# Mixed block pair with routed experts, 256 tokens: the first gather of the experts' stage spread over the first group's products, filler products during the routing, row splits on VectorE, one more weight tile

## The chip, the cores and the metric

The program runs on one core of a Trainium2 chip. TensorE (PE) multiplies, with its weight loads listed apart as PEld; VectorE (DVE), ScalarE (ACT) and GpSimd (POOL) do elementwise work; SyncE's queue (SP) issues the DMAs. The metric is the device time of one execution in microseconds (us), and the median of the runs counts. A profile is one further execution, recorded instruction by instruction.

## The reference

Two transformer blocks on 256 tokens of width 2048, all in float32. The first has two recurrent mixers, cross-attention and an MLP; the second has a gated mixer and, at the end, routed experts. Only the end matters for this change:

```python
x = x + gate1 * (y @ w_out[l])                       # end of the second mixer
h = rms_norm(x, norm2_g[l]) * (1.0 + scale2) + shift2
m = hierarchical_moe(h, ...)                         # 256 rows
x = x + gate2 * m

def hierarchical_moe(h, ...):                        # cut
    g_logits = hf @ w_group + b_group                # 4 groups, top 1
    e_logits = hf @ w_route + b_route                # 8 experts of that group, top 2
    weights = softmax(top_val) * p_group
    # rows sorted by expert; for each expert e and its rows xb:
    act = silu(xb @ w_gate[e]) * (xb @ w_up[e])      # 2048 -> 256
    ys = act @ w_down[e]                             # 256 -> 2048
    # out[n] = sum over its 2 experts of weights * ys
```

There are 32 experts with 2048x512 gate and up weights and 256x2048 down weights each. That is 6 MB an expert, so 192 tiles of 1 MB (128x2048 float32) are read.

## The kernel before

The stages run one after another: mixers, output product, cross-attention, MLP, the second block's mixer (`block2`), and the experts (`moe`). This text is about the seam between the last two and about `moe`.

**Routing and rows.** `route_piece` turns the rows of `h` into logits while `block2`'s last product ends. `moe` starts with `row_bcast` (32 small products that spread `gate2` over the partitions) and `route`, a long chain of short VectorE instructions: maxima, one-hots, counts by a few products of ones, ranks `rm`, weights `W`. `onehot` (L1639) makes from `rm` a matrix `oh` that picks the rows of a group of experts. `rows_hilo` normalizes the rows and splits them into `xh` (rounded, on ScalarE, L1656) and the remainder `xl`. For the first 128 tokens the remainder is made on GpSimd (L1661 and L1662), for the second 128 on VectorE (L1658). It does this for four column quarters q, so there are 8 `xh` and 8 `xl` instructions in all.

**Gather.** `gather` returns 8 pieces. Piece j makes two of the 16 column chunks of the gathered, transposed rows `xs`: eight products with `xh` and `xl` into one PSUM tile `mx` (two buffers), one drain on ScalarE (L1513) and one on VectorE (L1511). 

**Groups.** The 32 experts are in 9 groups, in most of which four experts have 32 rows each; such a group's four products sit side by side in TensorE's columns. `experts_in` makes gate and up of a group in four steps kg, one weight tile an expert in each. `experts_mid` applies the nonlinearity (L1579 to L1586) and `experts_out` makes the down products (tiles in two halves), scales them (L1610), splits them, and adds them to `h` (L1620). A float32 product appears in the trace as several instructions; a step kg of a four-expert group as 32, four at a time.

**Which expert is where.** The first group holds experts 0 to 3, whatever the routing. From the second group on, the experts stand in the order of their row counts, which `order` works out: some 16 VectorE instructions over 128x1024 elements (L1439 to L1446). It needs two work tiles `at` and `pr` of the tag `wh`, which has three buffers; its result `ids` (L1451) is read by SP's queue for the addresses of all loads from tile number 24 on.

**Weight tiles.** `load_ahead` issues the 192 loads in the order of their use, from SP's queue (L1714, L1721). Tiles 5, 6 and 7 go once into spare memory (an `xs` buffer and `wh`, `wl` buffers); the other tiles go round a ring of 9 slots: two in `b`, three `raw`, four `mw`. A load waits until the products on its slot's previous tile are done, and `take`, called before each kg and each half of the down products, issues what has become free by then. So 12 tiles are loaded ahead of the first group: its steps kg 0 to 2.

**Order of instructions.** The source is a sequence, and a scheduler decides at build time in which order each engine gets its instructions: the earlier in the source the higher the priority, but an instruction that the scheduler takes to be ready goes ahead of one that it takes to be waiting. On the chip each queue then runs in that fixed order. `keep_in_program_order` pins an instruction behind the one traced last on its engine.

Of the kernel before, what the change touches and what calls it, by code (L numbers as in the profile page):

```python
# [11 lines left out]
F32 = mybir.dt.float32  # L12
# [4 lines left out]
ALU = mybir.AluOpType  # L17
# [165 lines left out]
class Prog:  # L183
# [1463 lines left out]
    def rows_hilo(self, P):  # L1647
        nc = self.nc
        self.xh, self.xl = self.b16(F32R), self.b16(F32R)

        rs2 = self.smp.tile([128, 2], F32, tag="rs2", name="rs2", bufs=1)
        self.tc.keep_in_program_order(nc.vector.tensor_copy(rs2, self.rs))
        for q in range(4):
            for tb in range(2):
                c = self.cols(q)
                nc.scalar.activation(self.xh[:, tb, c], self.h[:, tb, c], AF.Copy, scale=self.rs[:, tb:tb + 1])  # L1656
                if tb:
                    nc.vector.scalar_tensor_tensor(self.xl[:, tb, c], self.h[:, tb, c], rs2[:, tb:tb + 1], self.xh[:, tb, c], ALU.mult, ALU.subtract)  # L1658
                else:
                    v = P.tile([128, 512], F32, tag="ey", name="xn", bufs=2)  # L1660
                    nc.gpsimd.tensor_scalar(v, self.h[:, tb, c], self.rs[:, tb:tb + 1], None, ALU.mult)  # L1661
                    nc.gpsimd.tensor_tensor(self.xl[:, tb, c], v, self.xh[:, tb, c], ALU.subtract)  # L1662


    def weights_init(self):
# [20 lines left out]


    def slot_tile(self, P, i):
        k = i % 9
        if k < 2:  # L1690
            if i == 0:
                self.pair = self.b16()
            w = self.pair[:, k]
        elif k < 5:
            w = self.rawp.tile([128, 2048], F32, tag="raw", name="raw")
        else:
            w = P.tile([128, 2048], F32, tag="mw", name="mw", bufs=4)
        return w

    def spare_tile(self, P, k):  # L1700
# [7 lines left out]
    def load_ahead(self, n, P=None):  # L1708
        while len(self.issued) < min(n, len(self.loads)):
            j = len(self.issued)  # L1710
            if 5 <= j < 8:
                w = self.spare_tile(P, j - 5)
                for x in range(2):
                    self.nc.sync.dma_start(w[x], self.loads[j]()[:, x * 1024:x * 1024 + 1024])  # L1714
            else:
                i = j if j < 5 else j - 3
                if (j - 12 if j < 17 else j - 9) >= self.used:
                    break
                w = self.slot_tile(P, i)
                if j < len(self.loads) - 4:  # L1720
                    self.nc.sync.dma_start(w, self.loads[j]())  # L1721
                w = self.halves(w)
            self.issued.append(w)

            if j == len(self.loads) - 1:
                for x in range(2):
                    for y in range(j - 3, j + 1):
                        self.nc.sync.dma_start(self.issued[y][x], self.loads[y]()[:, x * 1024:x * 1024 + 1024])
# [16 lines left out]
    def moe(self):  # L1745
        nc = self.nc
        with ExitStack() as ctx:
# [2 lines left out]
            self.row_bcast(self.modc[:, 5], self.g2row)  # L1750
            K = ctx.enter_context(self.tc.tile_pool(name="kept", bufs=1))
            P = ctx.enter_context(self.tc.tile_pool(name="moe", bufs=1))
            self.load_ahead(12, P)
            self.route(K)

            oh = self.onehot(P, [0], self.rm)
            self.rows_hilo(P)
            xs, work = self.gather(P, oh, 128)
            for w in work:
                w()  # L1760
            self.order(K)
            last = len(GROUPS) - 1
            st = self.group_in(P, 0, xs, oh, self.W, [[]] * 4)
            self.group_out(P, 0, st)
            oh = self.onehot(P, [1, 2], self.rmo)
            xs, work = self.gather(P, oh, 256)
# [3 lines left out]
            for g in range(1, last + 1):  # L1770
                i = (g - 1) % 2
                work = [[], [], [], []]
# [6 lines left out]
                c = slice(i * 128, i * 128 + 128)  # L1779
                st = self.group_in(P, g, [x[:, c] for x in xs], oh[:, :, c], self.Wo, work)  # L1780
# [5 lines left out]
                if i:  # L1786
                    oh, xs = oh2, xs2
            self.group_out(P, last, prev, last=True)
            n = nc.values_load(self.nov[0:1, 0:1], min_val=0, max_val=15)
            with self.tc.For_i(0, n, 1):  # L1790
                x = self.extra(P)
                xo, work = self.gather(P, x[0], 64)
                for w in work:
                    w()

                def load(src):
                    w = P.tile([128, 2048], F32, tag="mw", name="mw", bufs=4)
                    nc.sync.dma_start(w, src)
                    return self.halves(w)

                gu = lambda kg: [load(self.ins["wgu"][bass.ds(self.xe, 1), kg].rearrange("o p a c -> (o p) (a c)"))]
                halves = iter(range(2))
                dn = lambda: [load(self.ins["wd"][bass.ds(self.xe, 1), next(halves)].rearrange("o p c -> (o p) c"))]
                self.experts_out(P, self.block_in(P, gu, xo, *x), dn, last=True)
# [55 lines left out]
```

## Time and profile before

| | us |
|---|---|
| median of 3 runs | 2320.45 |
| lowest, highest | 2318.12, 2325.05 |
| the profiled execution | 2339.39 |
| its span | 2337.3 |

The profiled execution took 18.9 us more than the median; its span leaves out 2.1 us around the recorded work. Times inside the profile are counted from the span's start. An engine's busy time says little by itself; what matters is which wait ends last at each point.

### The profile page before, as it was taken

What the parts mean: (1) busy time and instruction counts of PE and PEld (TensorE: products, weight loads), DVE (VectorE), ACT (ScalarE), POOL (GpSimd) and SP (SyncE); (2) the same over time, 40 slices, a digit from 0 to 9 for tenths busy, and PEclk for the clock granted to TensorE, in tenths of its full rate; (3) what the DMA queues carried; (4) which work ended last, traced back from release to release, by engine and by line L of the source; (5) the groups of instructions that cost most, each with busy time, mean ns of one, the idle gap of its engine ahead of it and who ended that gap; (6) DMA issues with size and microseconds to landing.
All of it is one profiled execution on the core that took longest, in us unless ns stands there. A gap on an engine that the chain in (4) does not pass through costs nothing.

```text
span 2337.3 us, 40924 instructions
## 1 busy us (share of the span) xinstructions
PE 2198.2 (94%) x16672; PEld 1705.7 (73%) x16672; DVE 1507.6 (65%) x2557; ACT 893.2 (38%) x1445; POOL 70.6 (3%) x174
## 2 busy tenths in 40 slices
PE   6999999999999989999999999999999789888877
PEld 6988888888887779998998988987987432233222
DVE  5778887757678788777787787767657622222223
ACT  5444443444544445444444434445555210011000
POOL 1000000010000000000000000000000100000000
PEclk9999999999899999999999999999999799999999
DMA  7425443233268777887786787754445698999998
GB/s 244 150 94 179 157 164 130 82 105 110 73 234 303 284 274 258 278 306 267 264 315 248 261 318 258 260 186 153 166 161 196 250 386 336 405 388 420 420 421 336
DMA packets 101622, 575.18 MB, mean 246 GB/s; under 512 B 11548, under 2 KB 12700, under 8 KB 45880
## 3 DMA queue, kind: packets, MB, share of 16 engines
q1 hardware_dynamic: 101432, 572.55, 65.4%
q8 instruction: 132, 2.16, 0.4%
q14 instruction: 58, 0.48, 0.1%
HBM read 570.40 MB, written 2.10 MB: 245 GB/s over the span
## 4 chain that ended last, share of the span: by engine, by line
PE 78%; DMA 10%; DVE 8%; ACT 2%; issue 2%; SPq 0%; DVEq 0%; ACTq 0%
PE acc L250 44%; PE mx L250 32%; DMA mw<-wgu 3%; PE mx L254 2%; DMA raw<-wgu 2%; DMA raw<-wd 1%; DVE wl L290 1%; DMA mw<-wd 1%; DVE macc L830 1%; DMA mraw<-wmod 1%; DMA row<-wmod 1%; DMA b<-wgu 0%; DMA raw<-wout 0%; ACT wh L289 0%; DVE pr L1445 0%
## 5 line engine op out<-in xcount | busy, mean ns | idle before, releaser
L289 ACT CAST wh<-raw 128x1024 fp32r<-128x1024 f32 (+1 forms) x496 | 516.7, 1044 | 722.1 <-PE acc L250 517.4
L290 DVE TENSOR_TENSOR wl<-raw,wh 128x1024 fp32r<-128x1024 f32 (+1 forms) x496 | 599.9, 1214 | 202.3 <-ACT wh L289 199.9
L250 PE MATMUL acc<-b,wh 128*128 128x256 f32 x2560 | 467.5, 284 | 1.0 <-ACT b L367 1.0
L250 PE MATMUL mx<-b,wh 128*128 128x256 f32 (+1 forms) x2016 | 419.4, 298 | 0.7 <-ACT wh L289 0.7
L250 PEld LDWEIGHTS acc<-b,wh 128*128 128x128 f32 x2560 | 396.5, 189 | 3.2 <-ACT b L367 1.7
L250 PE MATMUL acc<-b,wl 128*128 128x256 f32 x1280 | 362.0, 283 | 0.0
L250 PEld LDWEIGHTS mx<-b,wh 128*128 128x128 f32 (+1 forms) x2016 | 324.4, 193 | 11.9 <-issue 3.3
L250 PE MATMUL mx<-b,wl 128*128 128x256 f32 (+1 forms) x1008 | 300.0, 298 | 0.3 <-DVE wl L290 0.3
L250 PEld LDWEIGHTS acc<-b,wl 128*128 128x128 f32 x1280 | 243.2, 190 | 0.7 <-DVE wl L290 0.4
L830 DVE SCALAR_TENSOR_TENSOR macc<-mraw,silc,macc 128x1024 f32<-128x1024 f32 x160 | 205.0, 1282 | 58.0 <-DMA mraw<-wmod 57.5
L250 PE MATMUL acc<-wh,fh 128*128 128x512 f32 x512 | 199.8, 390 | 0.0
L250 PE MATMUL acc<-wl,fh 128*128 128x512 f32 x512 | 199.6, 390 | 0.0
L250 PE MATMUL acc<-wh,fl 128*128 128x512 f32 x512 | 199.2, 389 | 0.0
L250 PEld LDWEIGHTS mx<-b,wl 128*128 128x128 f32 (+1 forms) x1008 | 193.5, 192 | 4.8 <-DVE wl L290 0.8
L250 PE MATMUL mx<-mw,xs 128*32 128x512 f32 (+1 forms) x448 | 127.5, 649 | 15.3 <-DMA mw<-wgu 15.3
L250 PE MATMUL acc<-wh,b 128*128 128x512 f32 x384 | 124.8, 403 | 1.0 <-ACT row L971 1.0
L250 PE MATMUL mx<-raw,xs 128*32 128x512 f32 (+1 forms) x344 | 105.7, 646 | 12.4 <-DMA raw<-wgu 12.4
L250 PEld LDWEIGHTS acc<-wl,fh 128*128 128x128 f32 x512 | 96.1, 188 | 20.8 <-DVE wl L290 1.0
L250 PEld LDWEIGHTS acc<-wh,fl 128*128 128x128 f32 x512 | 96.1, 188 | 19.8
L250 PEld LDWEIGHTS acc<-wh,fh 128*128 128x128 f32 x512 | 96.1, 188 | 19.8
L250 PE MATMUL mx<-b,xs 128*32 128x512 f32 (+1 forms) x240 | 92.1, 722 | 12.5 <-DMA b<-wgu 12.5
L1580 DVE SCALAR_TENSOR_TENSOR eth<-eth,mx 128x256 f32<-128x256 f32 x9 | 3.8, 421 | 150.5 <-ACT eth L1579 150.5
(481 smaller groups left out, 2802.0 us busy)
## 6 DMA issues: line engine op xcount, KB each, us to landing
raw<-w SPq DMA_DIRECT2D x128, 1024.0 KB, 5.7
mraw<-wmod SPq DMA_DIRECT2D x160, 512.0 KB, 5.0
raw<-win SPq DMA_DIRECT2D x76, 1024.0 KB, 4.8
mw<-wgu SPq DMA_DIRECT2D x54, 1024.0 KB, 11.0
raw<-wgu SPq DMA_DIRECT2D x42, 1024.0 KB, 12.3
b<-wgu SPq DMA_DIRECT2D x29, 1024.0 KB, 12.6
mw<-wd SPq DMA_DIRECT2D x26, 1024.0 KB, 12.3
raw<-wout SPq DMA_DIRECT2D x24, 1024.0 KB, 5.3
```

The costliest lines, as they stand in the source:

```text
L250: return self.nc.tensor.matmul(out, lhsT=lhsT, rhs=rhs, start=start, stop=stop, skip_group_check=True)
L254: return self.nc.tensor.transpose(out, in_, self.ident[:k, :k])
L289: nc.scalar.copy(h[:, :n], rs)
L290: nc.vector.tensor_tensor(l[:, :n], rs, h[:, :n], ALU.subtract)
L830: nc.vector.scalar_tensor_tensor(a, b, self.silc[:, k:k + 1], a, ALU.mult, ALU.add)
L1580: nc.vector.scalar_tensor_tensor(th[:n], th[:n], 1.0, ps[:n, 0:256], ALU.add, ALU.mult)
```

## The change

In `rows_hilo` all 8 remainders are made on VectorE; the 8 GpSimd instructions go. Ahead of them 8 products of ones with a constant (128x128 by 128x256, result unused) are put into TensorE's queue behind the routing's products. The ring gets a tenth slot, a fifth `mw` tile, and 13 tiles are loaded ahead, so the first tile of the first group's kg 3 is among them. The first gather's pieces no longer all stand ahead of the first group: pieces 0 and 1 stand ahead of kg 0, 2 and 3 ahead of kg 1, 4 and 5 ahead of kg 2, 6 and 7 and then `order` ahead of kg 3.

```diff
         self.tc.keep_in_program_order(nc.vector.tensor_copy(rs2, self.rs))
+        self.busy(8)
         for q in range(4):
             for tb in range(2):
                 c = self.cols(q)
                 nc.scalar.activation(self.xh[:, tb, c], self.h[:, tb, c], AF.Copy, scale=self.rs[:, tb:tb + 1])
-                if tb:
-                    nc.vector.scalar_tensor_tensor(self.xl[:, tb, c], ...)
-                else:
-                    v = P.tile([128, 512], F32, tag="ey", name="xn", bufs=2)
-                    nc.gpsimd.tensor_scalar(v, self.h[:, tb, c], self.rs[:, tb:tb + 1], None, ALU.mult)
-                    nc.gpsimd.tensor_tensor(self.xl[:, tb, c], v, self.xh[:, tb, c], ALU.subtract)
+                nc.vector.scalar_tensor_tensor(self.xl[:, tb, c], self.h[:, tb, c], rs2[:, tb:tb + 1], self.xh[:, tb, c], ALU.mult, ALU.subtract)
+    def busy(self, n):
+        ps = self.acc()
+        for _ in range(n):
+            self.tc.keep_in_program_order(self.mm(ps[:, 0:256], self.ones, self.c("run")))
...
-        k = i % 9
+        k = i % 10
...
-            w = P.tile([128, 2048], F32, tag="mw", name="mw", bufs=4)
+            w = P.tile([128, 2048], F32, tag="mw", name="mw", bufs=5)
...
-                if (j - 12 if j < 17 else j - 9) >= self.used:
+                if (j - 13 if j < 18 else j - 10) >= self.used:
...
-            self.load_ahead(12, P)
+            self.load_ahead(13, P)
...
             xs, work = self.gather(P, oh, 128)
-            for w in work:
-                w()
-            self.order(K)
             last = len(GROUPS) - 1
-            st = self.group_in(P, 0, xs, oh, self.W, [[]] * 4)
+            work.append(lambda: self.order(K))
+            st = self.group_in(P, 0, xs, oh, self.W, [work[0:2], work[2:4], work[4:6], work[6:9]])
```

## Rows read from the trace of the kernel before

**Rows 1.** The page: mean busy tenths of the DMA engines over 40 slices of the span.
```profile
DMA  7425443233268777887786787754445698999998
```

**Rows 2.** Busy time by stretch; the last three columns: TensorE's clock, DMA share, GB/s.
```profile
1826.00:1846.00 20.00, 19.64 (x88) 14.02 (x92) 5.57 (x12) 3.66 (x8) 0.00 (x0) 0.51 0.13 55
1900.00:1904.40 4.40, 4.40 (x37) 2.23 (x37) 0.55 (x1) 0.57 (x1) 0.00 (x0) 1.00 0.25 54
1949.00:1972.50 23.50, 22.46 (x90) 6.32 (x92) 5.11 (x16) 2.91 (x6) 0.00 (x0) 1.00 0.58 221
1996.00:2000.00 4.00, 4.00 (x44) 1.21 (x39) 0.00 (x0) 0.00 (x0) 0.00 (x0) 1.00 0.52 180
2048.00:2054.60 6.60, 6.60 (x62) 2.47 (x64) 0.00 (x0) 0.00 (x0) 0.00 (x0) 1.00 0.39 117
2054.60:2313.00 258.40, 216.31 (x1020) 67.55 (x1013) 67.25 (x119) 22.72 (x42) 0.00 (x0) 0.96 1.01 421
```

**Rows 3.** SP's queue in order of time: start, us, the loads issued.
```profile
1815.01 2.10 SPq L1721 DMA_DIRECT2D mw<-wgu  x4
1846.11 1.14 SPq L1721 DMA_DIRECT2D b<-wgu  x2
...
1863.70 11.75 SPq L1721 DMA_DIRECT2D raw<-wgu  x2
```

**Rows 4.** TensorE in order of time at the first group: start, us, count, idle before.
```profile
1813.95 3.92 PE L250 MATMUL mx<-cst,modc 128*128 128x128 f32 x32
1820.15 1.05 PE L250 MATMUL mx<-route,cst 128*128 128x64 f32 x8 [2.28 <-DVE route L1392]
...
1826.36 2.40 PE L250 MATMUL mx<-oh,b 128*128 128x128 f32 x10 [1.84 <-DVE b L1658]
...
1830.53 10.50 PE L250 MATMUL mx<-oh,b 128*128 128x128 f32 x48
...
1849.74 3.59 PE L250 MATMUL mx<-mw,xs 128*32 128x512 f32 x28
...
1858.37 0.62 PE L250 MATMUL mx<-raw,xs 128*32 128x512 f32 x1 [1.46 <-DMA raw<-wgu]
...
1868.80 0.69 PE L254 MATMUL mx<-cst,ea 128*128 128x128 f32 x2 [6.81 <-DVE ea L1582]
1870.00 1.06 PE L250 MATMUL acc<-raw,eat 128*32 128x512 f32 x1 [0.52 <-DVE eat L1586]
```

**Rows 5.** TensorE's clock as it fell: length, PE, PEld, DVE, ACT, POOL, clock, DMA.
```profile
1818.00:1822.00 4.00, 1.05 (x8) 0.97 (x8) 3.79 (x12) 3.32 (x7) 3.80 (x4) 0.97 1.02 414
1822.00:1826.00 4.00, 1.51 (x6) 1.35 (x6) 4.00 (x11) 0.43 (x1) 3.75 (x3) 0.50 1.01 426
```

**Rows 6.** VectorE in order of time: routing, `rs2`, then `order`.
```profile
1817.36 1.29 DVE L1412 TENSOR_TENSOR route<-route 128x8 f32<-128x8 f32 x1
...
1820.59 0.97 DVE L1417 TENSOR_TENSOR route<-route 128x8 f32<-128x8 f32 x1
...
1822.28 0.16 DVE L1418 TENSOR_TENSOR route<-route 128x8 f32<-128x8 f32 x1
...
1823.30 1.24 DVE L1652 COPY rs<-rs_y 128x2 f32<-128x2 f32 x1
...
1848.66 1.23 DVE L1439 TENSOR_TENSOR pr<-order 128x1024 f32<-128x1024 f32 x1 [6.69 <-PE mx L250]
...
1855.01 0.18 DVE L1451 CAST ids<-idf 128x32 int32<-128x32 f32 x1
...
1867.14 1.21 DVE L1446 TENSOR_REDUCE order<-pr 128x32 f32<-128x1024 f32 x1
```

**Rows 7.** By source line: a VectorE instruction like a remainder's, min/median/max in ns.
```profile
L1202 DVE SCALAR_TENSOR_TENSOR h<-h,rfr,xg x8: 741/745/747, 1761.3 to 1778.7; 128x512 f32<-128x512 f32 x8
```

**Rows 8.** TensorE's waits for weight tiles after the pauses of the stream.
```profile
1921.47 1.92 PE L250 MATMUL mx<-mw,xs 128*32 128x512 f32 x2 [1.44 <-DMA mw<-wgu]
...
2016.94 0.62 PE L250 MATMUL mx<-mw,xs 128*32 128x512 f32 x1 [1.43 <-DMA mw<-wgu]
```

More of the change, by code (lines that the diff above doesn't have):

```diff
@@ L1656, in rows_hilo @@
                 nc.scalar.activation(self.xh[:, tb, c], self.h[:, tb, c], AF.Copy, scale=self.rs[:, tb:tb + 1])
-                if tb:
-                    nc.vector.scalar_tensor_tensor(self.xl[:, tb, c], self.h[:, tb, c], rs2[:, tb:tb + 1], self.xh[:, tb, c], ALU.mult, ALU.subtract)
-                else:
-                    v = P.tile([128, 512], F32, tag="ey", name="xn", bufs=2)
-                    nc.gpsimd.tensor_scalar(v, self.h[:, tb, c], self.rs[:, tb:tb + 1], None, ALU.mult)
-                    nc.gpsimd.tensor_tensor(self.xl[:, tb, c], v, self.xh[:, tb, c], ALU.subtract)
+                nc.vector.scalar_tensor_tensor(self.xl[:, tb, c], self.h[:, tb, c], rs2[:, tb:tb + 1], self.xh[:, tb, c], ALU.mult, ALU.subtract)
[3 more added lines that the diff above has]
+            self.tc.keep_in_program_order(self.mm(ps[:, 0:256], self.ones, self.c("run")))
     def weights_init(self):
@@ L1796, in load @@
                 def load(src):
-                    w = P.tile([128, 2048], F32, tag="mw", name="mw", bufs=4)
+                    w = P.tile([128, 2048], F32, tag="mw", name="mw", bufs=5)
                     nc.sync.dma_start(w, src)
```

## Prediction

> **What bounds the kernel now.** I read the page first. Its slices show two regimes: over most of the span the DMA engines are partly idle, and in the last fifth they stand at 8 and 9 tenths [rows 1]. The change touches only the experts' stage, so I read that stage alone, in stretches. From 2054.6 to 2313 the DMA share is 1.01 at 421 GB/s [rows 2]: there the weights set the pace, and whatever starts the stream earlier ends it earlier. A 1 MB tile (1,048,576 bytes) takes 2.49 us at that rate. Before 2054.6 the stream stands still in five places. What the shares leave of each stretch is 0.87 of 1826 to 1846 (17.4 us), 0.75 of 1900 to 1904.4 (3.3 us), 0.42 of 1949 to 1972.5 (9.9 us), 0.48 of 1996 to 2000 (1.9 us) and 0.61 of 2048 to 2054.6 (4.0 us) [rows 2]. That is 36.5 us in all, the most that an earlier stream can give.
>
> Then the queue that issues the loads. After the four `mw` loads at 1815.01 nothing is issued until 1846.11 [rows 3]: the ring is full, and the next slot is free only when kg 0 of the first group is done with its tiles. TensorE's rows say why that is so late. The gather starts in earnest at 1826.36, having waited for VectorE's remainders; 48 of its 64 products take 10.50 us, 0.219 us each, and kg 0 follows at about 1841 [rows 4]. In that time the granted clock is 0.51, the lower level of 1.2 GHz [rows 2]. It fell at about 1822, after TensorE had done 1.05 us of work in the 4 us from 1818, while GpSimd was busy 3.80 us of them [rows 5]. Then comes a second place: the first group's kg 3 waits for tiles that were issued at 1846 (1.46 us at 1858.37), and its nonlinearity waits 6.81 us for VectorE, which is inside `order` from 1848.66 to about 1868 [rows 4, 6]. The down products start at 1870.0 [rows 4].
>
> **The change, part by part.**
>
> *Rows on VectorE.* Eight GpSimd instructions go, four VectorE instructions of 0.74 us come [rows 7]: 3 us more work on VectorE. But while GpSimd works, short VectorE instructions are stretched: 1.29 us at L1412, 0.97 at L1417 and 1.24 at L1652, against 0.16 us for L1418 on as few elements [rows 6]. The three give back 1.13 + 0.81 + 1.08 = 3.0 us. So `rs2` is ready at 1821.5 in place of 1824.5, and all eight remainders at 1821.5 + 5.9 = 1827.4. The first two, which pieces 0 and 1 need, are there by 1823. Bounds: if the stretching had another cause, `rs2` stays at 1824.5 and the remainders end at 1830.4; if more of the chain was stretched than these three, all is some 1 us earlier still.
>
> *Filler products.* I expect each of the 8 to appear as four instructions, and 32 such instructions took 3.92 us in `row_bcast` [rows 4]. The routing's products start 1.1 us earlier (L1412's excess), at 1819, and take 1.05 us; the fillers then run from 1820 to 1824. They cost TensorE nothing that it could use, since the remainders end only at 1827.4; without that cover they would cost 1 us (1823 to 1824). They leave about 1 us of idleness ahead of the routing's products where there were 2.28 us, and none where there were 1.84 us ahead of the gather [rows 4], so I take the clock to stay at 2.4 GHz; the other end is 1.2 GHz, a rival below.
>
> *Gather by pieces.* At the full clock I take half of 0.219 us a product, 0.9 us a piece. Pieces 0 and 1 are made by 1826; their drains on VectorE stand either between or behind the remainders, so kg 0 can start between 1825 and 1829. I take 1827.5. A step kg is 32 instructions, four abreast: 28 of them took 3.0 us at the full clock from 1849.74 on [rows 4], so 3.4 us. kg 0 is done at 1831 in place of 1846. After it come six pieces (5.3 us) and three steps (10.3 us): kg 3 ends at 1846.6, not at 1861.6. The drains of pieces 2 to 7 hide under the products of the step before.
>
> *Tenth slot.* The thirteenth tile is loaded when the twelfth is done, so the stream runs 2.5 us longer, from 1828.6 to about 1831, where kg 0 frees the next slots: the 17.4 us pause is gone or 1 to 2 us long. Tiles 13 to 15 for kg 3 land by about 1840, before kg 3 begins at 1843. One tile more in the ring is worth one tile's time at the last place where the ring was full: 2.5 us by the row. The Trainium skill puts a core's share of HBM at about 358 GB/s ("DMA: Bandwidth & Descriptors", Specifications); by that estimate the tile would be worth 2.9 us and the sum 0.4 us more. The trace's 421 GB/s [rows 2] does not agree, so 2.5 stands.
>
> *order moved.* It now stands behind pieces 6 and 7, but what holds it is the `wh` buffers, which tiles 6 and 7 of kg 1 occupy; before, it waited 6.69 us for them [rows 6]. kg 1 ends at about 1836, so `order` runs from 1836.5 to 1856.5 (20 us, as from 1848.66 to the last of it at 1867.14 + 1.21 and a short one). `ids` comes 6.5 us after its start [rows 6], at 1843, 12 us earlier than now. SP's queue is in order, and every load behind tile 23 waits for it, but the stream has static tiles until about 1857. The same VectorE queue then holds the drains of pieces 6 and 7 and the first group's nonlinearity. The latter is the open term: if it is queued behind all of `order`, the down products start at 1858; if it is queued where the products end, at 1846.6 + 2.9 = 1849.5. Against 1870 that is 12 or 20.5 us. Before, it stood at the very end of `order`; now the products end about 10 us after `order` begins where they ended 13 us after, so I take a place in the middle: 1854, 16 us earlier.
>
> **The sum.** From 1870 to 2054 TensorE is nearly always busy (22.46 of 23.5 us in the longest pause [rows 2]) and the pauses of the stream come from it, so this shift is carried on. Down products 16 us earlier, one slot 2.5 us. Then the waits for weights inside that stretch shrink: at 1918 to 1924 TensorE waits three times for tiles, 3.5 us in all, at 2002 to 2017 five times, 5.8 us (one of each place is shown), each time with a slower clock after it [rows 8]. A stream that is one tile further ahead saves up to 2.5 us at each; I take 3.5 us for the two. 16 + 2.5 + 3.5 = 22 us of the possible 36.5. The profiled execution would go from 2339.4 to about 2317; it stands 18.9 us above the median, and I carry the 22 us over as they are: 2320.45 - 22 = 2298.
>
> **Rivals.**
>
> *The clock falls all the same.* For it: it fell after less than 4 us with little work [rows 5], and TensorE's steps slow down again after the short waits at 1918 to 1924. Against it: the fillers close most of that gap. Pieces at 1.75 us and steps at 6.8 us put kg 0's end at about 1836; of the 31 us of half-clock work behind it 10 are done by 1846, where the clock is back in the rows of before [rows 2, 4], and the other 21 take 10.5: kg 3 ends at 1856.5. The stream pauses 5 us, the down products start near 1861: 9 + 2.5 us, 2309. The Trainium skill has this as a rule ("TensorE: Matmul & The Clock Gate", HAM oscillation): waits between bursts throttle TensorE again and each burst pays anew. The clock of 0.50 from 1822 [rows 5] agrees; whether the fillers suffice, no row here shows.
>
> *VectorE keeps the gain.* `order` stays whole ahead of the nonlinearity, or the scheduler draws the pieces together ahead of kg 0 again. Down products at 1858, or kg 0 at 1835 with the rest behind it: 12 + 2.5 us, 2306.
>
> *The later pauses take it back.* If TensorE, not the stream, sets 1930 to 1970 (its group with 96 and 64 rows has 22.46 us busy of 23.5 [rows 2]) and the row waits there are bound to the new order of drains, only what is beyond the slot's 2.5 us to 6 us arrives: 2315, within 0.3%.
>
> *Slower.* `order`'s 16 wide instructions are ready as soon as kg 1 is done, the drains of pieces 4 to 7 are not. If the queue has them ahead of those drains, TensorE stands until about 1857, kg 2 and 3 end at 1867 and not 1861.6, the stream pauses from 1844 to 1862, and the end is 5 us later: 2326. It decides from 15 us of such queueing on; each drain put behind one wide instruction alone costs 1.2 us. Against it: drains stand earlier in the source and so go first where both are ready.
>
> **How the numbers follow.** About 0.3% (7 us) is what a measurement of this kernel can tell from no change. Chances: the forecast, 17 to 32 us, 0.54; VectorE keeps the gain 0.21; the clock falls 0.12; the later pauses 0.08; slower 0.05. Faster by over 0.3% is 0.54 + 0.21 + 0.12 = 0.87, within it 0.08, slower 0.05. The range goes from 32 us (20.5 for the down products, 2.5 for the slot, 9 for all waits and their clock) to the clock's rival less 2 us: 2288 to 2311, which leaves out the last two cases and a little at the lower end.
>
> **What would show it.** Right: clock 1.00 from 1820 to 1846; first load after the thirteenth issued near 1831; no DMA pause of more than 2 us before 1880; `order` from about 1837; down products between 1850 and 1858; DMA share 1 from some 2030 on, the last tile 22 us earlier. Wrong: a clock of 0.5 through the pieces; the `ea` wait of 6.81 us grown to 10; drains of pieces 4 to 7 more than 2 us behind their products; a pause of the stream beyond 10 us anywhere. The forecast falls if the down products start after 1862.

## The result, and the profile after

The changed kernel takes 2299.21 us (median of 4 runs, 2297.77 to 2302.05), the kernel before beside it 2322.25 us (2318.12 to 2325.05): a ratio of 0.9889, with a 95% interval of 0.9858 to 0.9921, 23 us less. The forecast was 2298, with a range of 2288 to 2311.

**Reading two executions against each other.** The program up to the end of the second block's mixer is the same in both kernels, but it did not take the same time twice. I therefore split each profile at the start of the last of the 16 L1199 instructions (the output product of the second mixer), the *seam*. These two answers, by source line, show it as the last number of "first and last start": first before, then after.

```profile
L1199 DVE TENSOR_TENSOR xg<-acc,g x16: 680/684/692, 1759.5 to 1807.0; 128x512 f32<-128x512 f32 x16
```

```profile
L1199 DVE TENSOR_TENSOR xg<-acc,g x16: 678/682/692, 1736.0 to 1783.5; 128x512 f32<-128x512 f32 x16
```

So 23.5 of the 41.3 us between the two spans (2337.3 and 2296.0) lie ahead of the seam, where nothing was changed. Behind it, in what I call the *stage*, are 530.3 us before and 512.5 after. Times "behind the seam" below are counted from 1807.0 and 1783.5. A profile of each kernel taken again later has its seam at 1782.3 and 1796.2 and a stage of 532.2 and 508.6, so one stage is known to some 2 to 4 us; the mean gain of the two pairs is 531.25 - 510.55 = 20.7 us.

The page after, the DMA slices [rows 1]: 8 tenths stand in the slice in which the experts' stage begins, where there were 6; elsewhere a slice differs by a tenth at most.

```profile
DMA  7425443232278767887787787754445898999997
```

Busy time by stretch after; the columns are those of [rows 2]. The first stretch is the one that lies 19 to 39 us behind the seam, as the first there; the next four are the pauses that answer to the four there.

```profile
1802.50:1822.50 20.00, 17.31 (x148) 8.19 (x144) 14.24 (x20) 3.96 (x7) 0.00 (x0) 1.00 0.98 391
...
1861.50:1869.50 8.00, 8.00 (x52) 3.71 (x52) 2.18 (x4) 2.05 (x4) 0.00 (x0) 1.00 0.42 145
1917.50:1931.50 14.00, 13.29 (x55) 3.15 (x57) 3.01 (x12) 0.76 (x2) 0.00 (x0) 1.00 0.55 208
1953.50:1959.50 6.00, 6.00 (x57) 1.82 (x60) 0.77 (x3) 0.46 (x2) 0.00 (x0) 1.00 0.62 236
2007.50:2013.50 6.00, 6.00 (x57) 2.13 (x60) 0.00 (x0) 0.00 (x0) 0.00 (x0) 1.00 0.27 87
2013.50:2270.00 256.50, 216.09 (x1028) 68.02 (x1024) 67.19 (x119) 22.72 (x42) 0.00 (x0) 0.95 1.01 421
```

The first pause of the stream is gone: the DMA share is 0.98 where it was 0.13. The clock is 1.00 where it was 0.51; in the kernel before it had fallen just ahead of this stretch [rows 5]. The later four pauses are all still there: by the same reckoning as in the prediction they hold 4.6 + 6.3 + 2.3 + 4.4 = 17.6 us, against 19.1 before. Nearly the whole gain comes from the first place.

SP's queue after [rows 3]: five `mw` tiles, then the first slot that kg 0 frees, 23.3 us behind the seam where it was 39.1; the last row is the first load whose address comes from `ids`.

```profile
1792.36 2.59 SPq L1723 DMA_DIRECT2D mw<-wgu  x5
1806.81 0.80 SPq L1723 DMA_DIRECT2D b<-wgu  x2
...
1827.72 0.36 SPq L1723 DMA_DIRECT2D b<-wgu  x1
```

TensorE after, in order of time [rows 4]: the fillers, two pieces, kg 0, and so on to the first down product.

```profile
1795.58 1.05 PE L250 MATMUL mx<-route,cst 128*128 128x64 f32 x8 [0.35 <-DVE route L1414]
1796.46 3.70 PE L250 MATMUL acc<-cst 128*128 128x256 f32 x16
1799.81 2.08 PE L250 MATMUL mx<-oh,b 128*128 128x128 f32 x16
1801.83 0.62 PE L250 MATMUL mx<-b,xs 128*32 128x512 f32 x2
...
1804.02 0.62 PE L250 MATMUL mx<-b,xs 128*32 128x512 f32 x2 [1.12 <-DVE xs L1511]
...
1816.07 2.78 PE L250 MATMUL mx<-mw,xs 128*32 128x512 f32 x24 [0.84 <-DVE xs L1511]
...
1822.89 0.62 PE L250 MATMUL mx<-mw,xs 128*32 128x512 f32 x1 [1.12 <-DVE xs L1511]
...
1831.85 0.69 PE L254 MATMUL mx<-cst,ea 128*128 128x128 f32 x2 [5.46 <-DVE ea L1582]
1833.05 1.07 PE L250 MATMUL acc<-raw,eat 128*32 128x512 f32 x2 [0.52 <-DVE eat L1586]
```

VectorE after [rows 6]: the short instructions are short, the eight remainders stand in one run, `order` begins at 1810.63 and its last wide instruction stands just ahead of the nonlinearity `ea`. `ids` is there 33.9 us behind the seam (48.0 before), 10 us ahead of the load that needs it.

```profile
1794.06 0.16 DVE L1412 TENSOR_TENSOR route<-route 128x8 f32<-128x8 f32 x1
...
1798.05 0.16 DVE L1652 COPY rs<-rs_y 128x2 f32<-128x2 f32 x1
...
1798.25 5.39 DVE L1658 SCALAR_TENSOR_TENSOR b<-h,rs,b 128x512 fp32r<-128x512 f32 x8
1803.56 0.72 DVE L1511 TENSOR_SCALAR xs<-mx,A,modc 128x128 f32<-128x128 f32 x2
...
1810.63 1.23 DVE L1439 TENSOR_TENSOR pr<-order 128x1024 f32<-128x1024 f32 x1 [0.96 <-PE mx L250]
...
1817.37 0.17 DVE L1451 CAST ids<-idf 128x32 int32<-128x32 f32 x1
...
1829.59 1.22 DVE L1446 TENSOR_REDUCE order<-pr 128x32 f32<-128x1024 f32 x1
...
1831.32 0.47 DVE L1582 SCALAR_TENSOR_TENSOR ea<-eth,slw,mx 128x256 f32<-128x256 f32 x1
```

The eight remainders take 5.39 us together (a median of 0.744 us each, overlapping), as the like instruction of [rows 7] had it. The waits for tiles at the second group [rows 8] are 1.45 us twice after (1882.31 and 1884.80), against 1.44, 1.44 and 0.58 before.

### The profile page after: what moved, and what is told of

The parts are those of the page before. It is cut to its first block, busy times and chain, and to the rows that moved or that the text cites. A ratio compares the mean times of both kernels' runs of the same rounds, so it can differ in the third digit from the quotient of the medians.

```text
span 2296.0 us, 40946 instructions
## 1 busy us (share of the span) xinstructions
PE 2165.3 (94%) x16688; PEld 1681.5 (73%) x16688; DVE 1502.9 (65%) x2561; ACT 892.8 (39%) x1445; POOL 61.4 (3%) x166
## 4 chain that ended last, share of the span: by engine, by line
PE 75%; DMA 11%; DVE 9%; ACT 2%; issue 2%; SPq 0%; DVEq 0%; ACTq 0%
PE acc L250 43%; PE mx L250 30%; DMA mw<-wgu 4%; DMA mraw<-wmod 3%; DMA mw<-wd 2%; PE mx L254 2%; DVE wl L290 2%; DVE macc L830 1%; DMA row<-wmod 1%; DMA raw<-wd 1%; DMA b<-wgu 1%; ACT wh L289 0%; DMA raw<-wout 0%; DVE pr L1445 0%; DVE ey L1610 0%
## 5 line engine op out<-in xcount | busy, mean ns | idle before, releaser
L250 PE MATMUL mx<-b,wh 128*128 128x256 f32 (+1 forms) x2016 | 407.5, 292 | 0.7 <-ACT wh L289 0.7
L250 PEld LDWEIGHTS mx<-b,wh 128*128 128x128 f32 (+1 forms) x2016 | 314.9, 187 | 11.2 <-issue 3.3
L250 PE MATMUL mx<-b,wl 128*128 128x256 f32 (+1 forms) x1008 | 294.1, 292 | 0.8 <-DVE wl L290 0.8
L250 PEld LDWEIGHTS mx<-b,wl 128*128 128x128 f32 (+1 forms) x1008 | 188.2, 187 | 4.8 <-DVE wl L290 1.1
L250 PE MATMUL mx<-mw,xs 128*32 128x512 f32 (+1 forms) x512 | 122.8, 651 | 23.6 <-DMA mw<-wgu 21.7
L250 PE MATMUL mx<-raw,xs 128*32 128x512 f32 (+1 forms) x328 | 98.1, 644 | 10.4 <-DMA raw<-wgu 10.4
L250 PEld LDWEIGHTS mx<-mw,xs 128*32 128x32 f32 (+1 forms) x512 | 26.8, 119 | 89.0 <-issue 44.2
```

Source lines behind the costliest of these rows:

```text
L250: return self.nc.tensor.matmul(out, lhsT=lhsT, rhs=rhs, start=start, stop=stop, skip_group_check=True)
```

## The experiments

**One measure for all of them.** One number goes with the length of the stage in all kernels: the rate of the stream from 12 to 262 us behind the seam. First the kernel before, then the one after; the last column is GB/s.

```profile
1819.00:2069.00 250.00, 215.54 (x1106) 82.74 (x1106) 84.41 (x159) 32.56 (x60) 6.66 (x5) 0.91 0.86 350
```

```profile
1795.50:2045.50 250.00, 218.80 (x1191) 80.90 (x1192) 86.34 (x167) 33.97 (x63) 0.00 (x0) 0.97 0.94 384
```

With 421 GB/s as the full rate, the time lost is 250 x (1 - 350 / 421) = 42.2 us before and 22.0 after. In the table the stage less this loss is 488.0 to 490.5 us for all 14 profiles. So the stage is some 489 us and what the stream loses in its first 250 us. That is close to bookkeeping, since all kernels load the same 192 tiles: the measure says how much of the loss a part of the change removes, not by what cause. The ratios are to the kernel before on the same chip; kernels of one letter ran together on one chip.

| kernel | stage, us | GB/s | lost, us | stage less lost | first down product, behind seam | second group's `ea`, behind seam | ratio (95%) |
|---|---|---|---|---|---|---|---|
| before | 530.3 | 350 | 42.2 | 488.1 | 63.0 | 123.3 | 1 |
| after | 512.5 | 384 | 22.0 | 490.5 | 49.6 | 105.8 | 0.9889 (0.9858 to 0.9921) |
| A before again | 532.2 | 349 | 42.8 | 489.4 | 63.5 | 123.6 | 0.9998 (0.9983 to 1.0013) |
| A no fillers | 510.3 | 384 | 22.0 | 488.3 | 51.0 | 108.3 | 0.9915 (0.9889 to 0.9941) |
| A nine slots | 520.0 | 369 | 30.9 | 489.1 | 50.5 | 112.2 | 0.9943 (0.9919 to 0.9966) |
| A no pieces | 513.6 | 380 | 24.3 | 489.3 | 50.7 | 108.1 | 0.9918 (0.9884 to 0.9952) |
| B rows only | 527.3 | 356 | 38.6 | 488.7 | 59.3 | 119.9 | 0.9968 (0.9952 to 0.9984) |
| B ten slots only | 524.8 | 361 | 35.6 | 489.2 | 60.6 | 119.0 | 0.9960 (0.9938 to 0.9983) |
| B pieces only | 527.5 | 356 | 38.6 | 488.9 | 55.0 | 118.0 | 0.9961 (0.9941 to 0.9982) |
| B order split | 515.3 | 376 | 26.7 | 488.6 | 44.9 | 111.9 | 0.9891 (0.9851 to 0.9932) |
| C after again | 508.6 | 387 | 20.2 | 488.4 | 50.6 | 106.8 | 0.9936 (0.9916 to 0.9956) |
| C GpSimd rows | 511.9 | 381 | 23.8 | 488.1 | 51.0 | 107.1 | 0.9931 (0.9906 to 0.9956) |
| C rows and ten slots | 518.6 | 370 | 30.3 | 488.3 | 56.2 | 115.2 | 0.9945 (0.9928 to 0.9962) |
| C eleven slots | 499.3 | 402 | 11.3 | 488.0 | 48.7 | 101.7 | 0.9876 (0.9854 to 0.9899) |

**The kernel before again.** No edit; it gives the scatter of the measure.

> The kernel before, unchanged, for a second profile. Two lengths are read from each profile: the prefix, up to the last L1199 instruction at the seam (before 1806.4 us, after 1782.9 us), and the stage from there to the end of the span (before 530.9, after 513.1). Theory A: the change acts in the stage alone and the 23.5 us by which the two prefixes differ are one slow profiled execution of before; then this prefix is 1783 to 1790 and the stage 530 to 532. Theory B: the change also makes the earlier stages shorter (through the addresses of tiles and weights); then this prefix is again near 1806, and the times repeat 2318 to 2325.

Ratio 0.9998. The stage is 1.9 us longer than in the first profile, the first down product 0.5 us later; the repeated profile of the changed kernel, further below, is 3.9 us shorter in the stage. So I count as the kernel's own what goes beyond 2 us or so at a milestone and 4 us in a stage; two repeats are little to go by. The expectation counted from the start of the last pair of L1199 instructions, 0.6 us earlier than the seam. By that count this prefix is 1781.7 us, 1.3 below what theory A said and far from theory B's 1806: the 23.5 us ahead of the seam belong to one slow execution, not to the change.

**No filler products.**

```diff
-        self.busy(8)
```

> The changed kernel without the 8 filler products. Theory A (fillers hold the clock): TensorE's clock falls to 0.5 before or in the first pieces, each piece takes 1.75 us in place of 1.0 and each step of a group 6.8 in place of 3.4 us until it is back; kg 0 ends 4 to 5 us later, the order table starts as much later, the stage is 517 to 520 us. Rival: with GpSimd out of the way the gap in TensorE's work is only some 4 us and the clock stays; then the stage is 512 to 514, as with the fillers or 0.5 us shorter.

Neither theory came out: the clock does fall without them, but only for some 7 us, and the stage is 510.3 us. Three stretches of that kernel's trace (clock third from the right; kg 0 begins at 1806.03):

```profile
1806.00:1808.00 2.00, 1.97 (x9) 0.20 (x8) 2.00 (x4) 0.46 (x1) 0.00 (x0) 0.50 1.05 442
...
1810.00:1812.00 2.00, 2.00 (x16) 0.52 (x12) 0.00 (x0) 0.00 (x0) 0.00 (x0) 0.64 1.05 442
1812.00:1814.00 2.00, 2.00 (x21) 1.45 (x14) 0.00 (x0) 0.30 (x1) 0.00 (x0) 1.00 0.79 197
```

Down products 0.4 to 1.4 us later than in the two profiles of after (1.5 us counted from the routing's products, see below), the stage between theirs. As long as the pieces stand where they do, the fillers are worth nothing that shows in the stage.

**Nine slots.** The ring and the tiles ahead as before, all else as changed.

```diff
-        k = i % 10
+        k = i % 9
-                if (j - 13 if j < 18 else j - 10) >= self.used:
+                if (j - 12 if j < 17 else j - 9) >= self.used:
-            self.load_ahead(13, P)
+            self.load_ahead(12, P)
```

> The changed kernel with the ring of 9 slots and 12 tiles ahead of before. Theory A: the last tile lands one tile's time later, and the stage is 2.5 us longer than the changed kernel's, 515 to 516.5, with the first pause of the stream 2 to 4 us long instead of none. Rival 1: the waits of TensorE for weights in the second and fifth group grow by as much as well, 518 to 520. Rival 2: the slot is worth nothing, since TensorE sets the pauses, 513.

The down products come when they came (50.5), but the second group's nonlinearity is 5.4 to 6.4 us later and the stage 7.5 to 11.4 us longer. TensorE's waits for tiles at the second group have grown in both number and length (after: 1.45 twice):

```profile
1886.27 1.04 PE L250 MATMUL mx<-mw,xs 128*32 128x512 f32 x2 [2.50 <-DMA mw<-wgu]
1888.76 1.92 PE L250 MATMUL mx<-mw,xs 128*32 128x512 f32 x2 [1.45 <-DMA mw<-wgu]
1891.25 1.06 PE L250 MATMUL mx<-b,xs 128*32 128x512 f32 x1 [0.57 <-DMA b<-wgu]
```

Rival 1 was right. By these profiles the slot is worth three times and more the one tile (2.5 us) that the prediction gave it. The ratios are less sharp: 0.9943 here against 0.9889 and 0.9936 for the changed kernel in other sets of runs.

**No pieces.** The gather whole ahead of the first group, `order` behind it, all else as changed.

```diff
+            for w in work:
+                w()
+            self.order(K)
...
-            work.append(lambda: self.order(K))
-            st = self.group_in(P, 0, xs, oh, self.W, [work[0:2], work[2:4], work[4:6], work[6:9]])
+            st = self.group_in(P, 0, xs, oh, self.W, [[]] * 4)
```

> The changed kernel with the first gather whole ahead of the first group, as before, and the order table behind the gather. Theory A (the order table on VectorE, held by the buffers of kg 1's tiles, sets the down products): kg 0 ends some 6 us later, the stream pauses 4 to 6 us, but the order table starts only 6 us later and its nonlinearity stands further ahead in the queue, so the down products start 1 to 4 us later and the stage is 514 to 517. Rival (the restart of the stream sets all that follows): the stage is 518 to 520.

Stage 513.6, 1 to 5 us longer. kg 0 frees its slots 6 us later (29.4 behind the seam, where it was 23.3) and the stream pauses longer, but the clock stays at 1.00 through the gather. Alone, the pieces' removal costs little as well, as theory A had it.

**One part alone on the kernel before.** Rows on VectorE; the tenth slot; the pieces: each the part's lines of the diff above, on the kernel before.

> The kernel before with one part of the change alone: all remainders on VectorE, no GpSimd instructions. Lengths count from the last L1199 instruction at the seam to the end of the span (stage: before 530 and 532 in two profiles, changed kernel 512.5). Theory A (most of the gain before the down products comes from the routing that GpSimd no longer stretches): the gather begins 3 us earlier, the table and the down products start 5 to 9 us earlier, at 54 to 58 us in place of 63, and the stage is 521 to 526. Rival (fillers and pieces do it, each making up for the other where one alone is taken out): the clock falls as before, the down products start at 60 to 62 and the stage is 527 to 530.

> The kernel before with the tenth slot and 13 tiles ahead alone. Taking the slot out of the changed kernel cost 7.5 us. Theory A (the slot removes the waits of TensorE for tiles in the second group, wherever the stream is restarted): the down products start as before, at 62 to 63 us, the second group's nonlinearity 5 to 6 us earlier than before (118 against 123.3) and the stage is 523 to 526. Rival (one tile's time, 2.5 us, and the rest of the 7.5 only where the stream had restarted early): the second group's nonlinearity at 121 to 122, stage 527 to 529.

> The kernel before with the gather by pieces and the table behind it alone, GpSimd rows, no fillers, 9 slots. Theory A: kg 0 ends near 29 us and not 39, the stream pauses about 7 us and not 18, but at the lower clock the table's buffers come free only a few us earlier; the down products start at 59 to 61 and the stage is 526 to 529. Rival (the stream's restart sets what follows): the stage is 520 to 523.

Against the mean stage of before (531.2) they gain 4.0, 6.4 and 3.7 us, together 14.1 of the 20.7; the ratios, 0.9960 to 0.9968, give more, 7 to 9 us each, with intervals of some 4 to 5 us on either side. In all three the clock still falls and the stream still has a first pause. The rows came out as the rival had it (stage 527.3), the slot as theory A (524.8, second group's `ea` at 119.0). The pieces' stage, 527.5, is theory A's, but their down products came at 55.0, 4 us ahead of what it said: 8 us earlier than before, of which less than half is left in the stage. The filler products were not tried alone on the kernel before.

**`order` split.** The half behind `ids` (the wide instructions that reorder ranks, weights and counts) is queued behind the first group's nonlinearity.

```diff
-            work.append(lambda: self.order(K))
+            later = []
+            work.append(lambda: later.append(self.order(K)))
...
+            with self.tc.issue_after(self.last_on("DVE")):
+                later[0]()
```

> The changed kernel with the table in two halves: the part up to the expert numbers stays, the part that makes the ordered ranks and weights is queued on VectorE behind the first group's nonlinearity. Theory A (the down products wait for VectorE alone): the nonlinearity's input wait of 5.46 us falls under 2, the down products start at 44 to 46 us in place of 49.55 with the clock up, group 1's nonlinearity 3 to 5 us earlier than 105.8 and the stage is 507 to 510. Rival (what leaves the head of the queue comes back behind it: the second half delays the scaling of the down products): the stage is 511 to 514.

The wait for `ea` goes from 5.46 to 1.36 us and the down products come 4.7 us earlier than after. But the second group's nonlinearity is 6.1 us later: the rest of `order`, on which the second group's one-hots rest, now stands among the scaling of the down products. VectorE in order of time in this kernel (seam 1786.1):

```profile
1829.48 0.48 DVE L1585 SCALAR_TENSOR_TENSOR ea<-eth,slw,mx 128x256 f32<-128x256 f32 x1
...
1830.84 1.22 DVE L1445 TENSOR_TENSOR pr<-at,rm 128x1024 f32<-128x1024 f32 x1
...
1846.50 1.21 DVE L1446 TENSOR_REDUCE order<-pr 128x32 f32<-128x1024 f32 x1
```

What the wait at `ea` gives is taken back behind it: `order` ends at 1847.7, 61.6 us behind the seam, where it ended at 47.3. By the ratio (0.9891) it is no better than the changed kernel. So the 5.46 us at `ea` are not a gain that only had to be picked up, at least not by this split. Theory A was right up to the down products, and the stage came out behind even the rival's 511 to 514.

**The changed kernel again, and with GpSimd's rows.** The first is unaltered; in the second the remainders of the first 128 tokens are on GpSimd as before.

> The changed kernel unaltered, once more. If what the first profile of it shows is the kernel and not that one execution: stage behind the seam 512 to 513.5 us (512.5 before), down products of the first group 49.3 to 49.8 us behind the seam, second group's nonlinearity 105.5 to 106.2, ratio to the kernel before 0.986 to 0.992. A stage more than 2 us away from 512.5 would mean that differences of 2 us between my profiles tell nothing.

> The changed kernel with the remainders of the first 128 tokens on GpSimd again. Theory (removing GpSimd's stretching and GpSimd's own slow remainders is worth in the changed kernel what it was worth by itself on the kernel before, 3 to 5 us): down products 52.5 to 54 us behind the seam, stage 515 to 517.5, ratio 0.990 to 0.992. Rival (pieces and fillers cover it, since the first pieces need only the first remainders): down products at 50 to 51, stage 512 to 514, ratio as the changed kernel's.

After again: down products 37.51 us behind the routing's products, and 37.47 in the first profile (1795.58 to 1833.05 above). This part of the stage repeats to 0.1 us; only the seam's distance to the routing varies by 1 us. Counted so, the down products come at 39.0 without fillers, 38.8 without pieces and 45.0 without both. The stage missed what I expected by 3.4 us, and the ratio lies outside too, so the scatter is as wide as the single effects on after. With GpSimd back, so are the stretched instructions:

```profile
1797.08 1.28 DVE L1412 TENSOR_TENSOR route<-route 128x8 f32<-128x8 f32 x1
...
1800.30 0.96 DVE L1417 TENSOR_TENSOR route<-route 128x8 f32<-128x8 f32 x1
...
1801.99 0.15 DVE L1418 TENSOR_TENSOR route<-route 128x8 f32<-128x8 f32 x1
...
1803.01 1.25 DVE L1652 COPY rs<-rs_y 128x2 f32<-128x2 f32 x1
```

GpSimd in the same kernel, its subtractions (two inputs, L1663); between them stand its multiplications (one input):

```profile
1797.07 1.26 POOL L1663 TENSOR_TENSOR b<-xn,b 128x512 fp32r<-128x512 f32 x1
...
1799.96 1.27 POOL L1663 TENSOR_TENSOR b<-xn,b 128x512 fp32r<-128x512 f32 x1
...
1802.86 2.62 POOL L1663 TENSOR_TENSOR b<-xn,b 128x512 fp32r<-128x512 f32 x2
```

Each of the three long instructions begins under a subtraction and ends within 0.1 us of that subtraction's end. Not every one is held (L1415, with one input, took 0.20 us at 1800.06). L1418, which stands under a multiplication, takes 0.15 us. So it is not GpSimd's work as such that stretches by a microsecond, but its two-input instruction; under multiplications the longest is L1402 with 0.64 us.

kg 0 begins 1.8 to 2.8 us later, yet `order` and the down products only 0.5 to 1.5 us, since VectorE no longer has eight remainders ahead of the first drains (the 1.12 us wait at 1804.02 is gone). The fillers did not hold the clock here: behind a wait of 2.28 us ahead of the routing's products it fell at about 1801.5, and it was back at 1.00 from about 1805, while the fillers ran (1800.75 to 1806.14) and before the first piece was made:

```profile
1802.70:1804.70 2.00, 2.00 (x6) 1.63 (x5) 2.00 (x6) 0.00 (x0) 2.00 (x3) 0.50 0.98 414
1804.70:1806.70 2.00, 2.00 (x13) 1.77 (x13) 2.00 (x3) 0.00 (x0) 0.79 (x1) 0.93 1.04 438
```

The rival was right: in the changed kernel the rows are worth nothing that can be measured.

**Rows and ten slots, without pieces and fillers.** The edit of "no pieces" and that of "no fillers" together.

> The changed kernel without both the pieces and the filler products: rows on VectorE and the tenth slot remain. Theory (pieces and fillers do the same thing, each keeps the clock up or shortens what runs at the low clock, so that leaving out one costs nothing and leaving out both costs much): clock near 0.5 for 10 us and more ahead of step kg 0, down products 56 to 60 us behind the seam, stage 519 to 523, ratio 0.993 to 0.9955. Rival (neither is worth anything, rows and slot make the gain): down products at 51 to 52, stage 512 to 515, ratio 0.989 to 0.992.

Each of the two cost at most 5 us of stage when left out alone. Left out together they cost 5.6 to 6.6 us at the down products and 6.1 to 10 us in the stage, and the clock shows why. In that kernel's trace, by stretches (48 of the gather's products run from 1805.47 to 1815.97, and kg 0 in earnest from 1815.90):

```profile
1808.00:1810.00 2.00, 2.00 (x11) 2.00 (x11) 0.70 (x2) 0.46 (x1) 0.00 (x0) 0.50 0.87 365
...
1818.00:1820.00 2.00, 2.00 (x12) 0.39 (x8) 0.00 (x0) 0.00 (x0) 0.00 (x0) 0.50 0.00 0
1820.00:1822.00 2.00, 2.00 (x20) 0.56 (x16) 0.00 (x0) 0.00 (x0) 0.00 (x0) 0.81 0.00 0
1822.00:1824.00 2.00, 2.00 (x24) 0.58 (x20) 1.15 (x1) 0.00 (x0) 0.00 (x0) 1.00 0.86 274
```

The clock is 0.50 through these 48 products, during which TensorE is busy without a break, and rises while kg 0 runs. With pieces kg 0 comes sooner and with it the full clock; with fillers, and the rows on VectorE, the clock does not fall. By the ratios alone (0.9945 against 0.9936, one chip) this kernel and the changed one can't be told apart; it is the profiles, one of each execution, that do.

**Eleven slots.** One `mw` tile and one tile ahead more than in the change.

```diff
-        k = i % 10
+        k = i % 11
-            w = P.tile([128, 2048], F32, tag="mw", name="mw", bufs=5)
+            w = P.tile([128, 2048], F32, tag="mw", name="mw", bufs=6)
-                if (j - 13 if j < 18 else j - 10) >= self.used:
+                if (j - 14 if j < 19 else j - 11) >= self.used:
-            self.load_ahead(13, P)
+            self.load_ahead(14, P)
```

> The changed kernel with an eleventh slot (six mw tiles) and 14 tiles loaded ahead. Theory (the tenth slot was worth 7.5 us because the waits for weights in the second group shrank with it; 2.9 us of such waits are left there in the changed kernel): slot 2.5 us, waits 2.5 to 2.9 us, stage 505.5 to 508, ratio 0.985 to 0.9875. Rival 1 (only the slot itself counts): stage 510, ratio 0.988. Rival 2 (TensorE sets the pace up to the second group, the stream is ahead enough): stage 512 to 513, ratio 0.989.

2291.68 us against 2307.92 for the changed kernel on the same chip: 0.9876 (0.9854 to 0.9899) and 0.9936 (0.9916 to 0.9956) to the kernel before, intervals that don't meet. It beats both kernels. The stage, 499.3, is 9 to 13 us shorter than after's; I had expected 5 to 7. I had counted the slot and the waits at the second group. Counted from the routing's products, the second group's `ea` is 3.2 us earlier, the fifth group's 8 to 12. Place by place, the time that the stream loses (reckoned as above, stretches in us behind the seam):

| slots | 20 to 44 | 76 to 92 | 128 to 162 | 168 to 182 | 222 to 238 |
|---|---|---|---|---|---|
| nine | 4.7 | 5.4 | 14.0 | 1.4 | 4.8 |
| ten (after) | 1.4 | 5.4 | 7.3 | 2.6 | 4.6 |
| ten (after again) | 2.2 | 5.5 | 8.0 | 2.0 | 2.1 |
| eleven | 0.1 | 3.4 | 4.7 | 2.1 | 0.0 |

The third place, with nine, ten (after) and eleven slots:

```profile
1913.50:1947.50 34.00, 32.39 (x131) 9.12 (x134) 9.59 (x23) 4.15 (x8) 0.00 (x0) 1.00 0.64 248
```

```profile
1911.50:1945.50 34.00, 31.74 (x138) 8.71 (x136) 12.69 (x28) 4.32 (x8) 0.00 (x0) 1.00 0.82 330
```

```profile
1909.80:1943.80 34.00, 31.71 (x140) 9.63 (x139) 13.96 (x29) 3.80 (x7) 0.00 (x0) 1.00 0.90 363
```

The tenth slot takes off 2 to 3 us at the first place, 6 to 7 at the third and nothing at the second; the eleventh takes off 1 to 5 us at each place but the fourth.

## Why the prediction was right, point by point

**What bounds the kernel: right.** The stage follows the loss of the stream to within some 1.3 us in 14 profiles, and the first pause was the place that gave way. The step that a shift of the down products "is carried on" held for this change (13.4 us there, 17.5 at the second group, 19.8 at the last tile), but it is no rule: the pieces alone brought the down products 8 us and the stage 3.7, and the split of `order` brought them 4.7 us and a longer stage.

**The clock through the pieces: right, the reason half so.** It is 1.00 from the routing's products into the `ea` wait. But the prediction made the fillers the means and a fallen clock the price of their failure (a rival at 2309). Without them the clock fell and came back after 7 us, at a cost of 1.5 us at the down products and none that shows in the stage: it rose while kg 0 ran, and the pieces have kg 0 run early. Fillers and pieces are, by the profiles, two roads to the same thing: rows and ten slots without both lose 6 to 10 us of stage, without either one 0 to 5. The ratios don't show it (0.9945 without both, 0.9936 with both).

**Rows: right at the place, lost behind it.** `rs2` stands 0.16 us long, as said, and ends 2.8 us earlier behind the seam (3.0 said). Putting GpSimd back brings the 1.28, 0.96 and 1.25 us back, so the cause is shown; the prediction's "while GpSimd works" is too wide, it is GpSimd's subtractions. The Trainium skill has a rule for it ("SBUF — State Buffer", Who interferes with whom): VectorE and GpSimd share a pair of ports under an exclusive lock, and a VectorE instruction with two inputs in SBUF contends with GpSimd's reads. The stretched L1412 and L1417, with two inputs, agree. L1418 has two inputs as well and took 0.15 us under a multiplication that reads SBUF, and L1652, stretched, has one, so the rule as given here does not settle which instruction is held; which port was held no run shows. By themselves the rows gave 4.0 us of stage; in the changed kernel 1 us or so, within the scatter.

**Pieces and kg 0: right.** A piece took 1.0 us, not 0.9; the 8 fillers appear as 16 instructions, not 32, in 3.70 us, not 3.92. (The 32 instructions of `row_bcast` in [rows 4] are 16 products in the source, two instructions each.) The prediction's 3.0 us for 28 instructions of a step runs from the first start to the start of the next one, at 1852.74; the row's 3.59 runs to the end of the last. kg 1 took 3.6 us after (1808.66 to 1812.23), where 3.4 was said. kg 0 freed its slots 15.8 us earlier behind the seam (15 said), the next load after the thirteenth was issued at 23.3 behind it (24 said), and from 1794 to 1830 no stretch of 2 us had a DMA share under 0.72. kg 3 ended not 15 but 12.8 us earlier (1861.99 and 1825.67): drains stood behind the remainders once and behind wide instructions of `order` twice, and TensorE waited 1.12, 0.84 and 1.12 us. That is the mild form of the "slower" rival, at the 1.2 us a drain that it named; it did not come near the 15 us from which it decides.

**The open term: mis-sized by 2.6 us.** The down products are 13.4 us earlier (63.0 to 49.6), where 16 was taken between bounds of 12 and 20.5. The step that failed is "I take a place in the middle": `ea` stands at the very end of `order`, as before, so that the rival in which VectorE keeps the gain came true at this one place. The wait did not grow to 10 us, it is 5.46, since `order` itself began 14.5 us earlier. TensorE's clock falls at the end of this wait, as it did before: 0.57 in the 8 us from 1830.8 with 6.43 us busy, and 0.57 in the 8 us from 1866 before. The Trainium skill's rule that waits between bursts throttle TensorE again ("TensorE: Matmul & The Clock Gate", HAM oscillation) agrees here. Moving `ea` ahead by splitting `order` does not pay, as the split showed.

**The waits and the slot: the sum near, the terms wrong, so partly luck.** The prediction gave 2.5 us to the slot and 3.5 to shorter waits in two places. The waits did not shrink as forecast: at the second group they are 2.9 us where there were 3.5, at the later of the two places 6.4 (4.9 in the other profile of after) where there were 5.8. What changed at the second group is the clock. The same 10 us of the two kernels, before and after, each beginning where the group's first wait ends:

```profile
1919.00:1929.00 10.00, 7.98 (x30) 1.51 (x30) 0.00 (x0) 0.00 (x0) 0.00 (x0) 0.66 1.01 425
```

```profile
1882.30:1892.30 10.00, 8.01 (x42) 2.59 (x43) 1.32 (x3) 0.39 (x1) 0.00 (x0) 1.00 1.01 425
```

With the same busy time TensorE got 42 instructions done, not 30. So the second group's nonlinearity is 17.5 us earlier. In the groups behind it some 2 us more were gained: the last tile is used 19.8 us earlier behind the seam (506.1 to 486.3):

```profile
2313.14 0.62 PE L250 MATMUL acc<-raw,eat 128*32 128x512 f32 x1 [0.83 <-DMA raw<-wd]
```

```profile
2269.85 0.62 PE L250 MATMUL acc<-raw,eat 128*32 128x512 f32 x1 [0.82 <-DMA raw<-wd]
```

13.4, 4 and some 2 us thus stand where the prediction had 16, 3.5 and 2.5 (from the last tile to the end of the span it took 24.2 us before, 26.1 in this execution of after and 24.2 in its other one). But taking the slot away costs 7.5 to 11.4 us and adding another gives 9 to 13: the sentence "one tile more in the ring is worth one tile's time at the last place where the ring was full" is refuted; for the eleventh slot the two intervals of the ratio alone lie 0.0017, some 4 us, apart. One tile's time at every place where the ring runs full and then empty does not fit either: the table above has nothing at the second place for the tenth slot and 6 to 7 us at the third. Why the third gains so much was not tried. The errors of the terms have cancelled in part, and by the second measurement of the ratio (0.9936) the forecast's base of 2320.45 gives 2305.6 us: inside the range, but 7 us from the 2298.

**The later pauses.** They hold 17.6 us, 1.5 less than before, so the prediction's "no pause beyond 10 us anywhere" held and its hope for more of the 36.5 us did not. The rival in which they take the gain back did not occur: they stay, but do not grow in sum. The stretch at the full rate begins 17.6 us earlier behind the seam (247.6 to 230.0), where 24.6 was said (2030).

**What stays open.** The two measurements of the ratio, 0.9889 and 0.9936, have intervals that meet only at 0.9916 to 0.9921; 23 and 15 us. The part ahead of the seam took from 1781.8 to 1807.0 us over the profiles, with the program the same, and it carries that spread into every median. Why it varies was not studied.

## What to carry to other kernels

Where a stream of weights has the last word, look at every place where the ring of tiles runs full and then empty, and try one slot more: here a slot for a tile of 2.5 us was worth 6.4 to 13 us of stage, unevenly over these places, and more than any single change to the order of the work. Test a bundle of edits by leaving out pairs as well as single parts, since two that mend the same stall can each look worthless when removed alone. Split a long profile where the programs part before comparing: here the unchanged part differed by more than the gain.

## What the runs showed of the hardware

TensorE's clock, once at 1.2 GHz, did not rise while the gather ran, though TensorE was busy without a break: in the kernel with rows and ten slots 0.50 from 1802 to 1820, with weight loads 2.00 of 2.00 us in the stretches of the gather, and in the kernel before 0.51 from 1826 to 1846 [rows 2]. In each it rose while kg 0 ran: 0.81 in the stretch from 1820, kg 0 having begun in earnest at 1815.90; without fillers 0.64 in the stretch from 1810, kg 0 having begun at 1806.03. In the kernel with GpSimd's rows it rose while the filler products ran: 0.50 in the 2 us from 1802.70, 0.93 in the next. Why the gather did not bring it back was not tried by itself.

A filler product of 256 columns stands in the trace as two instructions and not four (16 in all, 3.70 us), so it is half as many instructions of nearly twice the length as the 32 of [rows 4].

Short VectorE instructions (0.16 to 0.23 us) took 0.96 to 1.34 us where they met a two-input instruction of GpSimd, and ended within 0.2 us of its end: so in all five kernels with GpSimd's rows, and in none without.
